# A one-core hybrid decoder layer: its order of issue made with the scheduler's detailed machine model

## The chip, the cores and the metric

The kernel runs on one core of one Trainium2 chip. The metric is the device time of one execution in microseconds (us), lower is better. Five engines work beside each other, each through a queue of its own: TensorE (PE) multiplies, VectorE (DVE) and ScalarE (ACT) do elementwise work, GpSimd (POOL) does almost nothing here, and SyncE (SP) issues DMA transfers; ACT issues some too. Each queue is a fixed list, made when the kernel is built, and an instruction that waits for another engine holds up what stands behind it in its list.

## What is computed

A decoder layer over 2048 rows of 1024 numbers. Two mixing groups read one normalised projection, their outputs go through one output projection, and a gated FFN follows. All is float32. Cut to what matters:

```
h = rms_norm(x, pre_mix_norm)
proj = h @ w_in                       # lru_x, lru_gate, ssd_z, ssd_x, B, C, dt
lx = conv4(lru_x)
lh = rg_lru(lx, ...)                  # gates, then a scan over time
y_lru = rms_norm(lh * gelu(lru_gate))
xbc = silu(conv4(ssd_x, B, C))
dt = softplus(ssd_dt + bias)
y = ssd_chunked(x * dt, dt * A, B, C) # chunks of 128 rows, decays by running sums of dt * A
y_ssd = rms_norm((y + d * x) * silu(ssd_z))
x = x + rms_norm(concat(y_lru, y_ssd) @ w_out)
h = rms_norm(x, pre_ffn_norm)
x = x + rms_norm((silu(h @ w_gate) * (h @ w_up)) @ w_down)
```

## The kernel before

Each float32 operand of a product is split in two: `s_hi`, a cast to the matmul's type on ACT (L132), and `s_lo`, what that cast left out, on DVE (L133). A product is then three matmuls per tile, hi by hi (L137), hi by lo (L138) and lo by hi (L139), on tiles of 128 x 512. The FFN takes seven products where a plain block scheme takes eight, so it works on sums of weight halves (`S`) and on operands built by casts `hx` and `hy` (L717, L718).

The mixing half works on two time blocks of 1024 rows. A block runs its SSD units, eight of them in two groups of four, then its eight LRU units. A unit begins with projections of 48 matmuls each into a PSUM tile `pp` (pool of two); PE does the mixing itself into tiles `pq` (another pool of two). The stretches, as the trace shows them: start 0 to 50 us, SSD of block 0 to 340, LRU of block 0 to 550, the same for block 1 to 830 and 1020, output projection to 1362, FFN gate and up products to 2205, FFN down products to 2634.

The code is written unit by unit, and the Tile framework's scheduler turns it into the five queues: it keeps each dependence and decides, with a model of what instructions cost, which of the ready ones is put next on each engine. The kernel's author steers it in places by a higher priority (`HQ`) and by places (`site`) at which a mixing stage is written between two halves of a projection; no order is written out by hand.

Names that matter below, in the order of the program. At the start three projections (dt, B and C of block 0) run on raw x, since the row norm isn't known yet; L620 squares x on ACT and L167 makes the operands `hx`. L158 spreads the row norms over the partitions on PE and ACT copies them to `rsb`, which every later projection of block 0 is multiplied by on DVE (L295, writing `xr`, from which the convolution reads: L299 on ACT, then taps L302 on DVE). Right behind that copy the code loads eight tiles of x rows for block 1's norm (L632, on SP) and squares them on ACT (L633):

```
rms_of(acc, rtok[:, 0])
a.copy(out=rsb, in_=spread(rtok[:, 0], 0, NC, t4()))                      # L627, L158 within
...
        sy.dma_start(out=xr, in_=x[r0:r0 + P, :])                         # L632
        a.activation(out=xr, in_=xr, func=AF.Square, accum_out=ss[...])   # L633
```

L422 transposes the dt rows into a `pq` tile. The decay chain follows: L443, L447 (running sums on PE), L449 (copy to `Bt` on DVE), a write to DRAM `cs_dr`, loads L511 that spread a row of it over all partitions (`L`), and then per unit: L514 transposes x on PE, L516 and L518 make `t4` from it on DVE, L524 and L525 turn `L` into exponents on DVE, L530 (PE) multiplies `t4`, and L535, L542, L546, L551 carry the chunk states. L118 sums squares over partitions on PE at a block's end. L243, L244 and L172 make operands of later projections.

At 1362 to 1400 the output projection's last rows and the FFN's first products overlap: L717 and L718 build operands, L132, L735 split weights and sums of weights, L917 copies a product out, L920 and L921 (silu) work on it.

## Time and profile before

| what | value |
|---|---|
| time, median of 3 runs | 2635.73 us (2632.55 to 2636.6) |
| the profiled execution's own time | 2635.64 us |
| its span | 2633.8 us |
| PE busy | 2613.7 us, 99% |
| DVE busy | 1852.7 us, 70% |
| ACT busy | 1123.6 us, 43% |
| mean granted TensorE clock | 0.999 of full speed |

The span goes from the first to the last instruction. The profile of this kernel is read on two scales: over the whole, where PE is always busy, and at single places, where the row of time of one engine shows how long it stood still before an instruction and what released it.

### The profile page before, as it was taken

The page shows a single profiled execution, that of the slowest core. Times are in us where ns is not written, and L with a number is a line of the kernel's source. Part 1 is how long each engine was busy: PE and PEld are TensorE (multiplying, and loading weights), DVE is VectorE, ACT ScalarE, POOL GpSimd, SP SyncE. Part 2 cuts the span into 40 slices and gives each one's busy share as a digit, 9 for nine tenths or more (in the row PEclk, how much of TensorE's full clock was granted, in tenths as well). Part 3 has the DMA queues.
Part 4 walks back from the last instruction along what each step waited for, and adds up shares of the span by engine and source line. Part 5 has one row for each costly group of instructions (what it writes and reads, how often), then busy time and mean ns, then how long its engine had stood idle before and what let it go on. Part 6 is the DMA issues. An engine that isn't in the chain of part 4 may idle for free.

```text
span 2633.8 us, 31866 instructions
## 1 busy us (share of the span) xinstructions
PE 2613.7 (99%) x12360; PEld 2170.4 (82%) x12360; DVE 1852.7 (70%) x2716; ACT 1123.6 (43%) x1340; POOL 1.1 (0%) x8
## 2 busy tenths in 40 slices
PE   9999999999999999999999999999999999999998
PEld 7888888888888887888877888888888888888887
DVE  7997878888777767544478777678767675334676
ACT  6544456754535777332253222234222222322443
POOL 0000000000000000000000000000000000000000
PEclk9999999999999999999999999999999999999999
DMA  5342461223334635543454333235333325444664
GB/s 211 111 131 73 128 201 65 82 88 113 95 96 150 210 96 205 154 136 123 143 196 150 134 104 116 81 121 195 104 100 110 106 92 173 151 139 153 212 245 140
DMA packets 189975, 357.79 MB, mean 136 GB/s; under 512 B 18528, under 2 KB 91616, under 8 KB 189824
## 3 DMA queue, kind: packets, MB, share of 16 engines
q1 hardware_dynamic: 88912, 256.56, 30.3%
q10 hardware_dynamic: 100912, 99.20, 10.8%
q8 instruction: 97, 1.59, 0.2%
q14 instruction: 54, 0.44, 0.1%
HBM read 253.86 MB, written 101.84 MB: 135 GB/s over the span
## 4 chain that ended last, share of the span: by engine, by line
PE 93%; DVE 3%; ACT 2%; DMA 1%; issue 1%; DVEq 0%; ACTq 0%; SPq 0%
PE pf L139 16%; PE pf L138 16%; PE pf L137 16%; PE pp L137 11%; PE pp L139 10%; PE pp L138 10%; PE pq L137 3%; PE pq L138 3%; PE pq L139 3%; PE pq L530 1%; PE pq L542 1%; PE pq L551 1%; DMA t_dr<-L 1%; PE pq L514 1%; DVE t L399 0%
## 5 line engine op out<-in xcount | busy, mean ns | idle before, releaser
L137 PE MATMUL pp<-hx,s_hi 128*128 128x512 f32 x1392 | 548.2, 394 | 1.2 <-ACT hx L243 0.7
L139 PE MATMUL pp<-hx,s_lo 128*128 128x512 f32 x1392 | 545.4, 392 | 0.5 <-DVE s_lo L133 0.5
L138 PE MATMUL pp<-hx,s_hi 128*128 128x512 f32 x1392 | 543.6, 391 | 0.6 <-DVE hx L244 0.6
L132 ACT CAST s_hi<-raw 128x1024 fp32r<-128x1024 f32 (+1 forms) x167 | 170.3, 1022 | 380.2 <-PE pp L138 123.0
L139 PEld LDWEIGHTS pp<-hx,s_lo 128*128 128x128 f32 x1392 | 261.7, 188 | 56.5 <-issue 0.9
L137 PEld LDWEIGHTS pp<-hx,s_hi 128*128 128x128 f32 x1392 | 261.8, 188 | 56.2 <-issue 1.6
L138 PEld LDWEIGHTS pp<-hx,s_hi 128*128 128x128 f32 x1392 | 261.9, 188 | 54.2 <-DVE hx L244 1.0
L139 PE MATMUL pf<-hx,s_lo 128*128 128x512 f32 x704 | 273.9, 389 | 0.7 <-DVE s_lo L133 0.7
L137 PE MATMUL pf<-hx,s_hi 128*128 128x512 f32 x704 | 274.2, 389 | 0.4 <-ACT s_hi L132 0.4
L138 PE MATMUL pf<-hx,s_hi 128*128 128x512 f32 x704 | 273.9, 389 | 0.0
L133 DVE TENSOR_TENSOR s_lo<-raw,s_hi 128x1024 fp32r<-128x1024 f32 (+1 forms) x167 | 198.0, 1187 | 64.1 <-ACT s_hi L132 55.7
L978 DVE TENSOR_TENSOR d_lo<-draw,d_hi 128x1024 fp32r<-128x1024 f32 (+1 forms) x110 | 121.5, 1129 | 171.4 <-ACT d_hi L977 170.1
L132 ACT CAST s_hi<-S 128x1024 fp32r<-128x1024 f32 x86 | 90.3, 1050 | 268.6 <-PE pf L138 247.3
L138 PE MATMUL pf<-d_lo,d_hi 128*128 128x512 f32 x504 | 196.1, 389 | 0.0
L977 ACT CAST d_hi<-draw 128x1024 fp32r<-128x1024 f32 (+1 forms) x110 | 104.9, 980 | 213.5 <-PE pf L138 181.6
L139 PE MATMUL pf<-d_hi,d_lo 128*128 128x512 f32 x504 | 195.9, 389 | 0.0
L137 PE MATMUL pf<-d_hi 128*128 128x512 f32 x504 | 194.6, 389 | 0.0
L139 PEld LDWEIGHTS pf<-hx,s_lo 128*128 128x128 f32 x704 | 132.1, 188 | 28.9 <-DVE s_lo L133 1.6
L137 PEld LDWEIGHTS pf<-hx,s_hi 128*128 128x128 f32 x704 | 132.1, 188 | 28.2 <-ACT s_hi L132 0.9
L138 PEld LDWEIGHTS pf<-hx,s_hi 128*128 128x128 f32 x704 | 132.1, 188 | 27.4
L302 DVE SCALAR_TENSOR_TENSOR lx<-xr,pk,lx 128x1024 f32<-128x1024 f32 x108 | 138.2, 1279 | 10.4 <-ACT lx L299 9.3
L138 PE MATMUL pf<-hy,s_hi 128*128 128x512 f32 x356 | 138.8, 390 | 1.5 <-DVE hy L718 1.4
(339 smaller groups left out, 4518.2 us busy)
## 6 DMA issues: line engine op xcount, KB each, us to landing
raw<-w_gu_dram SPq DMA_DIRECT2D x86, 512.0 KB, 4.2
f_dr<-fo ACTq DMA_DIRECT2D x154, 256.0 KB, 4.5
raw<-w_in_dram SPq DMA_DIRECT2D x72, 512.0 KB, 3.4
draw<-f_dr SPq DMA_DIRECT2D x57, 512.0 KB, 4.3
L<-cs_dr SPq DMA_DIRECT2D x32, 512.0 KB, 5.3
g_dr<-t ACTq DMA_DIRECT2D x32, 512.0 KB, 3.4
raw<-g_dr SPq DMA_DIRECT2D x32, 512.0 KB, 5.0
raw<-h_dr SPq DMA_DIRECT2D x26, 512.0 KB, 4.4
```

What stands on the lines that cost most here:

```text
L132: a.copy(out=hi, in_=raw)
L133: v.tensor_sub(out=lo, in0=raw, in1=hi.bitcast(F32))
L137: te.matmul(o, lhsT=wh, rhs=hi, start=start, stop=False)
L138: te.matmul(o, lhsT=wh, rhs=lo, start=False, stop=False)
L139: te.matmul(o, lhsT=wl, rhs=hi, start=False, stop=stop)
L302: v.scalar_tensor_tensor(out=y, in0=xr[:, k:k + TB], scalar=cw(k), in1=y, op0=ALU.mult, op1=ALU.add)
L514: te.transpose(pt[:, c].rearrange("p j d -> p (j d)"), xc[:, c * P:(c + 1) * P], ident)
L530: te.matmul(pst[:, c, :], lhsT=Bt[:, c, :], rhs=xe[:, c].rearrange("p j d -> p (j d)"), start=True, stop=True)
L542: te.matmul(po[:, c, :], lhsT=(sc[:, xi, :] if c == 0 else U[:, c - 1, :]), rhs=C[:, c * P:(c + 1) * P], start=True, stop=True)
L551: te.matmul(py[64 * j:64 * j + 64, c, :], lhsT=xd[:, c, j, :], rhs=L[:, j, c, :], start=True, stop=True)
L977: a.copy(out=hi, in_=r)
L978: v.tensor_sub(out=lo, in0=r, in1=hi.bitcast(F32))
```

## The change

One argument of the framework's context changes. It lets the scheduler weigh its choices on a simulated timeline of the machine in place of a coarser count:

```
-    with tile.TileContext(nc) as tc:
+    with tile.TileContext(nc, schedule_with_timeline_sim=True) as tc:
```

Both kernels have the same 16,501 instructions on the same tiles; loads of ACT's function tables go from 105 to 100, and waits are placed anew. On PE the order differs strongly up to 400 us (mixing matmuls, `pq`, stand further behind the projections, `pp`; 45 matmuls of projections go ahead of L158), a little up to 850, at 980 to 1110, at 1362 to 1400 and at 2200 to 2530, and not at all over 1400 to 2200. SP puts an eighth weight load ahead of the x rows (L632) where it put seven. Three places follow.

ACT's queue at 42 to 56 us, as the difference of the two orders (`t_465` to `t_477` are tiles of x rows, `Cc` and `lx` convolutions):

```order
-L132 CAST s_hi<-raw 128x1024
-L627 COPY rsb<-pq 128x1024
 L633 ACTIVATE t_465,h_ss<-t_465 128x1024
-L299 ACTIVATE lx<-xr,pk 128x1024
 L633 ACTIVATE t_466,h_ss<-t_466 128x1024
 L633 ACTIVATE t_467,h_ss<-t_467 128x1024
-L299 ACTIVATE Cc<-xr,pk 128x1024
+L627 COPY rsb<-pq 128x1024
+L132 CAST s_hi<-raw 128x1024
 L633 ACTIVATE t_468,h_ss<-t_468 128x1024
 L633 ACTIVATE t_477,h_ss<-t_477 128x1024
+L299 ACTIVATE lx<-xr,pk 128x1024
```

The copy to `rsb` has gone behind three squares of x rows, and the first convolutions behind two more.

DVE's queue around the first unit's decays, at 82 to 96 us, before (numbers tell tiles apart):

```order
L449 COPY Bt_580<-pq_571 16x1024
L490 TENSOR_TENSOR SM_611<-pq_602,tri_138 128x1024
L302 SCALAR_TENSOR_TENSOR lx_855<-xr_853,pk_109,lx_855 128x1024 x2
L516 TENSOR_TENSOR t4_760<-pq_751,dt_525 128x1024
L302 SCALAR_TENSOR_TENSOR lx_855<-xr_853,pk_109,lx_855 128x1024
L518 TENSOR_TENSOR t4_762<-t4_760,ed_585 128x1024
L524 TENSOR_TENSOR L_748<-L_748,cs_583 128x2048
L535 SCALAR_TENSOR_TENSOR t4_835<-sc_149,aet_588,pq_826 128x64
L525 TENSOR_SCALAR L_748<-L_748 128x2048
```

and now:

```order
L449 COPY Bt_580<-pq_571 16x1024
L133 TENSOR_TENSOR s_lo_1073<-raw_1070,s_hi_1072 128x1024
L490 TENSOR_TENSOR SM_611<-pq_602,tri_138 128x1024
L524 TENSOR_TENSOR L_748<-L_748,cs_583 128x2048
L302 SCALAR_TENSOR_TENSOR lx_855<-xr_853,pk_109,lx_855 128x1024
L516 TENSOR_TENSOR t4_760<-pq_751,dt_525 128x1024
L524 TENSOR_TENSOR L_954<-L_954,cs_583 128x2048
L525 TENSOR_SCALAR L_748<-L_748 128x2048
L302 SCALAR_TENSOR_TENSOR lx_855<-xr_853,pk_109,lx_855 128x1024
L518 TENSOR_TENSOR t4_762<-t4_760,ed_585 128x1024
L525 TENSOR_SCALAR L_954<-L_954 128x2048
```

The first L524 stands ahead of L516 and L518 of its unit where it stood behind them, and a second L524, that of the next unit, is there too.

PE's queue where the mixing of block 0's seventh unit begins, at 266 to 270 us, before:

```order
L542 MATMUL pq_2104<-Cc_1574,sc_149 128x128
L542 MATMUL pq_2104<-Cc_1574,t4_2021 128x128 x7
L551 MATMUL pq_2116<-L_1934,t4_1946 64x128 x16
L514 MATMUL pq_2144<-ident_113,lx_2041 128x128 x8
L137 MATMUL pp_2164<-hx_214,s_hi_1960 128x512
```

and now, from the row behind L551 on:

```order
L139 MATMUL pp_2256<-hx_341,s_lo_2053 128x512
L137 MATMUL pp_2256<-hx_345,s_hi_2052 128x512
L138 MATMUL pp_2256<-hx_346,s_hi_2052 128x512
L139 MATMUL pp_2256<-hx_345,s_lo_2053 128x512
L137 MATMUL pp_2256<-hx_349,s_hi_2052 128x512
L138 MATMUL pp_2256<-hx_350,s_hi_2052 128x512
L139 MATMUL pp_2256<-hx_349,s_lo_2053 128x512
L137 MATMUL pp_2256<-hx_353,s_hi_2052 128x512
L138 MATMUL pp_2256<-hx_354,s_hi_2052 128x512
L139 MATMUL pp_2256<-hx_353,s_lo_2053 128x512
L137 MATMUL pp_2405<-hx_214,s_hi_2167 128x512
L514 MATMUL pq_2144<-ident_113,lx_2041 128x128 x8
```

The transposes L514 into `pq_2144` stood right behind L551; now eleven matmuls of projections stand between.

## Rows read from the trace of the kernel before

**Rows 1.** The page: busy us (share), instructions; the chain's shares; one matmul group.

```profile
PE 2613.7 (99%) x12360; PEld 2170.4 (82%) x12360; DVE 1852.7 (70%) x2716; ACT 1123.6 (43%) x1340; POOL 1.1 (0%) x8
...
PE 93%; DVE 3%; ACT 2%; DMA 1%; issue 1%; DVEq 0%; ACTq 0%; SPq 0%
...
L138 PE MATMUL pp<-hx,s_hi 128*128 128x512 f32 x1392 | 543.6, 391 | 0.6 <-DVE hx L244 0.6
```

**Rows 2.** FFN stretch: its length, each engine's busy us (instructions), clock, DMA.

```profile
1500.00:1600.00 100.00, 100.00 (x443) 82.81 (x442) 71.49 (x102) 28.92 (x38) 0.00 (x0) 1.00 0.28 95
```

**Rows 3.** PE's timeline: start, us, instruction, [idle before, releaser].

```profile
269.25 1.06 PE L514 MATMUL pq<-ident,lx 128*128 128x128 f32 x8 [1.75 <-DVE t L546]
...
389.06 0.50 PE L138 MATMUL pq<-t,bd 128*128 128x512 f32 x1 [0.78 <-DVE t L378]
...
547.51 1.95 PE L118 MATMUL pq<-ones,acc 128*128 128x1 f32 x16 [0.97 <-DVE acc L322]
...
1002.11 0.50 PE L138 MATMUL pp<-hx,s_hi 128*128 128x512 f32 x1 [0.56 <-DVE hx L244]
...
1011.10 0.50 PE L137 MATMUL pp<-hx,s_hi 128*128 128x512 f32 x1 [0.67 <-ACT hx L243]
```

**Rows 4.** Stretches behind two of these stalls; the clock stands third from the end.

```profile
551.00:555.00 4.00, 4.00 (x12) 3.09 (x12) 3.76 (x21) 3.11 (x5) 0.00 (x0) 0.60 0.36 131
...
268.00:274.00 6.00, 4.75 (x25) 4.13 (x26) 5.96 (x6) 0.24 (x1) 0.00 (x0) 1.00 0.82 240
```

**Rows 5.** ACT's timeline around rsb.

```profile
48.11 1.02 ACT L627 COPY rsb<-pq 128x1024 f32<-128x1024 f32 x1 [4.77 <-PE pq L158]
50.69 1.06 ACT L633 ACTIVATE t<-t 128x1024 f32<-128x1024 f32 x1 [1.56 <-DMA t<-x_dram]
```

**Rows 6.** The chain at 44 us; transfer rate over 0 to 75 us.

```profile
44.07 6.59 DMA t<-x_dram
...
GB/s 5 221 337 397 388 405 398 404 400 420 409 256 11 0 4 48 232 0 0 0 0 0 4 249 205 323 393 417 411 417 422 223 24 0 0 0 0 0 9 0
```

**Rows 7.** PE's timeline, start and decay chain.

```profile
49.27 1.07 PE L422 MATMUL pq<-ident,Bt 128*128 128x128 f32 x8
...
79.61 0.46 PE L443 MATMUL pq<-dtx,tri 128*128 128x128 f32 x2 [1.14 <-DVE halo L300]
```

**Rows 8.** DVE's timeline behind the decay chain; SP's loads; the page on them.

```profile
82.18 1.21 DVE L449 COPY Bt<-pq 16x1024 f32<-16x1024 f32 x1 [1.26 <-PE pq L447]
...
90.98 1.27 DVE L302 SCALAR_TENSOR_TENSOR lx<-xr,pk,lx 128x1024 f32<-128x1024 f32 x1
92.17 1.22 DVE L518 TENSOR_TENSOR t<-t,ed 128x1024 f32<-128x1024 f32 x1
93.31 2.28 DVE L524 TENSOR_TENSOR L<-L,cs 128x2048 f32<-128x2048 f32 x1
...
95.80 1.22 DVE L525 TENSOR_SCALAR L<-L 128x2048 f32<-128x2048 f32 x1
...
85.33 1.76 SPq L511 DMA_DIRECT2D L<-cs_dr  x4
...
L<-cs_dr SPq DMA_DIRECT2D x32, 512.0 KB, 5.3
```

**Rows 9.** Stretches of block 0; DVE's busy time is the third.

```profile
100.00:120.00 20.00, 20.00 (x127) 16.91 (x125) 18.80 (x28) 11.88 (x11) 0.00 (x0) 1.00 0.34 106
...
220.00:240.00 20.00, 20.00 (x129) 17.14 (x128) 13.78 (x27) 9.18 (x9) 0.00 (x0) 1.00 0.12 37
```

**Rows 10.** The chain: one product in two units of block 0.

```profile
127.39 1.90 PE pq L551 x32
...
155.80 1.90 PE pq L551 x32
```

**Rows 11.** PE's timeline where the FFN begins.

```profile
1380.61 0.50 PE L138 MATMUL pf<-hy,s_hi 128*128 128x512 f32 x1 [1.16 <-DVE hy L718]
...
1390.74 0.50 PE L137 MATMUL pf<-hx,s_hi 128*128 128x512 f32 x1 [0.44 <-ACT s_hi L132]
```

## The prediction

> **What bounds the kernel now.** I read the page's busy shares first, then its chain of work, then TensorE's own row of time, since a new order can only win where an engine that sets the end stands still. PE is busy 2613.7 us of a span of 2633.8, and the chain that ended last is 93% PE [rows 1]. The reader is to see two things there. First, all idle time of PE together is 2633.8 − 2613.7 = 20.1 us, 0.76% of the span: no order of the same instructions can win more than that, apart from what the clock gives. Second, VectorE is at 70% over the whole, so wherever it is much fuller than that it can become what PE waits for.
>
> Next I read the stretches. In the FFN (1362 to 2634 us) PE is busy 100.00 us of 100 and issues 443 matmuls in them [rows 2], one every 0.226 us; DVE stands at 71.49 there. No order can help in it. The Trainium skill, "Perfetto Trace Analysis", section "Identifying the Most-Contended Engine", says that matmul busy time is a poor measure of how near TensorE is to its limit and takes weight-load busy time in its place; that is 82.81 of 100 in the same row, which by the Trainium skill would leave 17% of room. The row decides for me: PE waits nowhere in that stretch, so the room, if there is any, is not one that an order opens.
>
> What is left are PE's stalls, and these are few [rows 3]. The idle time before a matmul, which the timeline puts in brackets, is 1.75 us at 269.25 (eight transposes of the mixing stage wait for VectorE's L546), 0.78 at 389.06 (and as much again at 510.95 us), 0.97 at 547.51, 0.56 at 1002.11 and 0.67 at 1011.1 us. Behind the one at 547.51 the granted clock is 0.60 over 551 to 555 us, while behind the longer one at 269 it stays at 1.00 [rows 4]. The start of the kernel is the other place where PE waits for something other than PE.
>
> **The change part by part.** Instructions, tiles and pools stay; only the place of each instruction in its engine's queue changes. An engine takes its queue in turn, so what matters is who now stands behind whom. The profiled execution took 2635.64 us, of which 2633.8 are span and 1.8 lie outside it; the median of the three runs is 2635.73, so sums made on the trace carry over as they stand.
>
> *Gains.* In the new order the projection's matmuls (pp) stand ahead of the mixing stage's (pq) that wait for VectorE: at 269 us, 11 matmuls of 0.226 us now stand between L551 and the transposes, and the L542 whose result L546 reads are begun earlier too, and counted in PE work the wait's end is far behind. I walked each of the six stalls against the new queues, and all six have their releaser done before PE arrives. Idle time 1.75 + 0.78 + 0.78 + 0.97 + 0.56 + 0.67 = 5.5 us [rows 3]; the first matmul after a stall also takes 0.50 us [rows 3] where such matmuls take 0.391 on average [rows 1], which makes 0.1 each and 6.2 in all. If the clock's fall at 551 goes with the stall before it, 4 us × (1 − 0.60) = 1.6 us more [rows 4].
>
> *Start.* On ACT, L627 (the copy that makes rsb, the row norms spread over all partitions) ran at 48.11 us, and the first square of an x row (L633) at 50.69, having waited 1.56 us for its DMA [rows 5]. Now three squares stand ahead of L627. The first row lands at 44.07 + 6.59 = 50.7 us [rows 6]; rows of 512 KB at some 410 GB/s [rows 6] follow 1.28 us apart, so the third lands at 53.2. The square takes 1.06 us and L627 1.02 [rows 5], so rsb is ready at about 55.4 rather than 49.1. SyncE's queue also has one more weight load ahead of these rows, which puts up to 1.28 us on it: 55.4 to 56.7, and I take 56.1, 7 us later.
>
> What covers that? PE moves 45 projection matmuls (10.2 us) ahead of L158, whose result rsb copies, so PE is at its transposes L422 at about 53.1 and not at 49.27 [rows 7], with that much more of its later work done. They need rsb (it frees their PSUM buffer): a stall of 56.1 − 53.1 = 3.0 us, 2.3 to 3.6 by the bounds above. Everything on VectorE that multiplies by rsb (L295) moves late by about 7 us too.
>
> *The decay chain.* By the walk PE's L447 of the first block ends at 93.0, and L449 takes 1.21 us [rows 8]. From L449's end at 83.39 it was 1.94 us to SyncE's loads L511 (issued 85.33), which take 5.3 to land [rows 8]: L is there at 94.2 + 1.9 + 5.3 = 101.4 us. Before, VectorE did L516 and L518, of which the next PE product L530 is made, and then L524, the first to need L. Now L524 stands ahead of L516, so L518 waits for the load, and two L524 (2.28 each), one L525 (1.22), two L302 (1.27), L516 and L518 (1.22, both of one shape) [rows 8] are 10.8 us and make it end at about 112.2; PE arrives at 108.1 by the walk: a stall of 4.1 us, or 4.7 if its load waits for a weight load's tail. The wait of 1.14 us at 79.61 [rows 7] goes, with its slow first matmul 1.3. To these comes 0.2 us at the very start, where a square (L620) steps ahead of the first L167. Start and decay chain: 0.2 + 3.0 + 4.4 − 1.3 = +6.3 us.
>
> *What follows.* VectorE cannot win this back soon: it is busy 18.80 of 20 us at 100 us, about the same in each 20 us up to 200, and 13.78 at 220 [rows 9]. One unit of the SSD loop took 155.80 − 127.39 = 28.4 us [rows 10]. By the new queues the loop from one L295 to the next is a projection of 48 matmuls (10.9 us) and some 1.8 us of mixing on PE, then about 16.8 us on VectorE, an estimate from the durations above: 29.3 us. That puts 0.9 us on each of the first two units, before VectorE has room: +1.8. So the first block loses 8 us; I hold 5 to 11 for it, from 2.3 of stall and no growth to a growth over five units.
>
> *Output projection to FFN, 1378 to 1396.* The casts of hy go ahead on both engines, so the gap of 1.16 us at 1380.61 [rows 11] and three smaller ones in the 5 us behind it go, 2.4 us in all by my count of that stretch. But the cast L132 of the FFN's first weight sums, which ended a wait of 0.44 us at 1390.74 on PE [rows 11], now stands behind the silu L921 of a later product. PE is there at 1387.2 by the walk and is served at about 1390.7: 3.5 us, with 0.6 for the second half 4.1, of which 1.3 (this wait, the like one at 1392 and their slow first matmuls) were there before. Net 4.1 − 1.3 − 2.4 = +0.4, bounds −1.3 and +2.
>
> *Rest.* New small waits in the LRU stage and the second block, where the walk leaves under 1.5 us of slack: +1, bounds 0 and +2.5.
>
> *The clock.* The new stalls are of 3, 4 and 3.5 us. Behind the stall of 0.97 us at 547.51 the clock fell for 1.6 us' worth; behind 1.75 us at 269 it did not [rows 3, 4]. The Trainium skill, "TensorE: Matmul & The Clock Gate", section "HAM oscillation — how this bites in real kernels", has idle gaps on PE bring the clock back down, which speaks against this change: it trades several short gaps for few long ones. By the rule all three would pay 1.6 us; the trace agrees at 547 and not at 269. By the rows, then, each pays 0 or 1.6, and I take one of three in full.
>
> **The sum.** −6.2 − 1.6 + 8 + 0.4 + 1 + 1.6 = +3.2 us, by the bounds −3 to +13. On 2635.7 that is 2639.
>
> **The rivals.** *It is slower beyond what can be measured.* One mechanism: rsb late, VectorE behind it and full until 200 us. If the loop's 29.3 us hold through five units and not two, the loss of the first block is 11 us, and if the clock falls behind all three stalls another 3.2: +3.2 + 3 + 3.2 = +9.4, 2645; with both PE stalls at their far ends 2648. For it speaks that VectorE has 1.2 us to spare in 20; against it that some VectorE work (L133 for weights far ahead) has room to slip. It decides from where PE at 230 us is more than 10 us behind the old order.
>
> *It is faster.* If PE has enough finished projections to run over the late rsb (its two pp buffers and the 45 matmuls speak for it, the two buffers' release by L295 against it), the start costs 2 us and not 8: −3, about 2633, not yet measurable; with VectorE's order closer than I walked and no clock fall −6 or more, 2627 to 2630. A third would be that PE's matmuls themselves run closer together, by more than the 20.1 us of idle: under 2614. That is what the Trainium skill's measure of headroom would allow; nothing in the rows supports it, and I give it 1 in 100.
>
> *It does nothing.* The queues in the FFN and the tail keep their order on PE, half the kernel, and PE always has the same 2613.7 us of work. Then gains and losses cancel to within 2 us: 2634 to 2638. The forecast differs from it only by size.
>
> **How the numbers follow.** About 0.2% (5.3 us) is what a measurement of this kernel can tell from no change: 2630.5 to 2641. My forecast, a small loss inside that band, together with the case of nothing, holds 0.49; the slower rival 0.40; faster beyond the band 0.11. The likeliest time is 2639. The range runs from 2629 (half of the faster case) to 2650 (the far end of the slower one); the likeliest case alone would be 2633 to 2643.
>
> **What would show it.** In the trace after: rsb (L627) ends at 55 to 57 us and not at 49.1; PE has a stall of about 3 us before L422 and one of about 4 before the first L530; a stall of about 3.5 us near 1390; none at the six places above; VectorE over 95% busy to about 240 us; the lag of PE against the old order some 8 us at 230, some 3 at 1400 and unchanged to the end. I am wrong if rsb comes before 52 us, if VectorE keeps pace so that the lag at 230 is under 4 us, or if the FFN stretch, with PE's order the same, takes another time than 443 matmuls in 100 us.

## The result, and the profile after

The new order takes 2662.1 us (median of 4 runs, 2661.2 to 2663.4) against 2635.8: a ratio of 1.0103, interval 1.0085 to 1.012. It is 26.4 us slower. The sign was the forecast's, a loss; the size was not, and the time lies outside the range.

The page of the new order, with the lines that answer to [rows 1]: busy us (share) and instructions by engine, then the chain by engine.

```profile
span 2659.4 us, 31893 instructions
...
PE 2622.9 (99%) x12360; PEld 2179.0 (82%) x12360; DVE 1849.9 (70%) x2716; ACT 1124.9 (42%) x1335; POOL 1.1 (0%) x8
...
PE 91%; DVE 4%; ACT 2%; DMA 2%; issue 1%; ACTq 0%; SPq 0%; DVEq 0%
```

The shares hardly changed, and PE still reads 99%. Two differences make up the whole result. PE stands still for 2659.4 − 2622.9 = 36.5 us where it was 20.1, +16.4. And the same matmuls keep it busy for 2622.9 us where it was 2613.7, +9.2, since some run at the lower clock. Together 25.6 us, the difference of the spans.

PE's timeline of the new order, all idle times over 1.5 us after the first 55 (start, us, instruction, [idle before, releaser]); it answers to [rows 3, 7 and 11]:

```profile
55.25 1.06 PE L422 MATMUL pq<-ident,Bt 128*128 128x128 f32 x8 [1.52 <-ACT rsb L627]
...
110.05 3.42 PE L530 MATMUL pq<-t,Bt 128*128 128x128 f32 x16 [3.63 <-DVE t L518]
...
145.35 0.50 PE L137 MATMUL pp<-hx,s_hi 128*128 128x512 f32 x1 [2.32 <-DVE xr L295]
...
345.67 0.79 PE L137 MATMUL pp<-hx,s_hi 128*128 128x512 f32 x1 [4.10 <-DVE xr L295]
...
405.68 0.73 PE L137 MATMUL pq<-t,bd 128*128 128x512 f32 x2 [2.96 <-ACT t L377]
...
407.92 0.79 PE L137 MATMUL pp<-hx,s_hi 128*128 128x512 f32 x1 [1.51 <-DVE t L308]
...
1056.86 0.73 PE L137 MATMUL pq<-wob,s_hi 128*128 128x512 f32 x2 [2.93 <-ACT wob L243]
...
1414.19 0.80 PE L137 MATMUL pf<-hx,s_hi 128*128 128x512 f32 x1 [4.88 <-ACT s_hi L132]
```

These eight are 23.9 us of idle time. The old order had none over 1.75 in these stretches.

Stretches of the new order (length, busy us of PE, PEld, DVE, ACT, POOL with their instructions, clock, DMA share, GB/s); they answer to [rows 2, 4 and 9]:

```profile
100.00:120.00 20.00, 16.37 (x80) 13.99 (x79) 20.00 (x17) 8.16 (x6) 0.00 (x0) 0.91 0.33 108
120.00:140.00 20.00, 20.00 (x123) 16.67 (x121) 13.35 (x24) 5.71 (x6) 0.00 (x0) 1.00 0.51 132
...
220.00:240.00 20.00, 20.00 (x98) 16.81 (x97) 19.25 (x18) 13.06 (x11) 0.00 (x0) 1.00 0.28 93
...
110.00:114.00 4.00, 3.95 (x21) 3.90 (x22) 4.00 (x4) 3.04 (x3) 0.00 (x0) 0.63 0.00 0
...
146.00:150.00 4.00, 4.00 (x19) 3.30 (x18) 4.00 (x7) 2.04 (x3) 0.00 (x0) 1.00 0.39 131
346.00:350.00 4.00, 4.00 (x13) 3.15 (x13) 4.00 (x6) 2.07 (x3) 0.00 (x0) 0.69 0.25 81
...
406.00:410.00 4.00, 2.49 (x7) 1.69 (x6) 4.00 (x6) 3.35 (x4) 0.00 (x0) 0.56 0.48 135
410.00:414.00 4.00, 4.00 (x12) 3.09 (x12) 4.00 (x6) 3.25 (x4) 0.00 (x0) 0.58 0.95 331
1057.00:1061.00 4.00, 3.43 (x9) 2.43 (x10) 2.65 (x5) 3.65 (x5) 0.00 (x0) 0.68 0.96 325
...
1415.00:1419.00 4.00, 4.00 (x10) 3.09 (x10) 4.00 (x6) 1.03 (x2) 0.00 (x0) 0.50 0.33 123
...
1600.00:1700.00 100.00, 100.00 (x443) 82.81 (x442) 71.34 (x102) 29.40 (x37) 0.00 (x0) 1.00 0.27 93
```

The last row is that of [rows 2] again: 443 matmuls in 100 us, the FFN is untouched. Behind the stalls of 2.9 us and more the clock is low; behind 2.32 at 145 it is not in this trace (the last section has others). The loss (1 − clock) × 4 us is 1.5 at 110, 1.2 at 346, 3.4 at 406 to 414, 1.3 at 1057 and 2.0 at 1415, with the two stretches behind the last two (0.89 and 0.84) another 1.1: 10.5 us. The 1.6 at 551 in the old order is gone, which leaves 8.9, about the 9.2; part of the slow clock lies in idle time, where it costs nothing.

To see where the time was lost I compared, matmul by matmul, when the two traces had issued the same amount of PE work. The difference is PE's *lateness*; it changes only where one of the kernels stalls or runs slow. "Lateness" below is always this number, worked out from one trace of each kernel. Matmuls of unlike size have to be weighed for it, so it is good to some 0.3 us, and two executions of one order can differ by more, as the last section shows.

| stretch, us | lateness at its end | change | predicted |
|---|---|---|---|
| 0 to 225 | 9.6 | +9.6 | +8 (start) |
| 225 to 325 (stall at 269 gone) | 7.7 | −1.9 | a gain |
| 325 to 375 | 13.9 | +6.2 | in "Rest" |
| 375 to 400 | 14.4 | +0.5 | in "Rest" |
| 400 to 425 (here the product that waited at 389) | 21.0 | +6.6 | in "Rest", and a gain |
| 425 to 550 | 19.7 | −1.3 | a gain |
| 550 to 600 (clock at 551) | 16.8 | −2.9 | a gain |
| 600 to 1000 | 17.7 | +0.9 | in "Rest" |
| 1000 to 1050 | 16.4 | −1.3 | a gain |
| 1050 to 1100 | 21.8 | +5.4 | in "Rest" |
| 1100 to 1400 | 21.7 | −0.1 | 0 |
| 1400 to 1450, then flat to the end | 25.3 | +3.6 | +0.4 |

The gains came: 1.9 + 1.3 + 2.9 + 1.3 = 7.4 us where the sum had 6.2 + 1.6 = 7.8, of which 0.9 was for the wait at 389. That product comes at 419 in the new order and doesn't wait, but its gain cannot be seen apart beside the loss at 405. The start came in size. What the sum had put at +1, the "Rest", is +6.2 + 0.5 + 6.6 + 0.9 + 5.4 = 19.6 us: three places of which the prediction knew nothing, at 345, 405 and 1057 us.

**345 us.** DVE's and ACT's timelines of the new order, where PE waits for L295:

```profile
340.92 1.23 DVE L370 TENSOR_TENSOR SM<-L,bd 128x1024 fp32r<-128x1024 f32 x1 [5.62 <-ACT bd L365]
342.06 1.22 DVE L322 TENSOR_TENSOR acc<-acc,t 128x1024 f32<-128x1024 f32 x1
343.20 1.28 DVE L302 SCALAR_TENSOR_TENSOR lx<-xr,pk,lx 128x1024 f32<-128x1024 f32 x1
344.39 1.22 DVE L295 TENSOR_TENSOR xr<-pp,rsb 128x1024 f32<-128x1024 f32 x1
```

```profile
329.72 1.40 ACTq L362 DMA_DIRECT2D L<-wa_dram  x2
...
338.99 1.90 ACT L365 CAST bd<-L 128x2048 fp32r<-128x2048 f32 x1 [10.33 <-DMA L<-wx_dram]
```

The gate weights of the LRU stage are loaded into `L`, a tile that the SSD stage's decays use too. The loads are issued 29 us later than in the old order, where the cast L365 ran at 312.0:

```profile
300.49 1.40 ACTq L362 DMA_DIRECT2D L<-wa_dram  x2
```

The new order kept the cast and its user at the head of their queues all the same: ACT stands 10.33 us, DVE 5.62, and L295, which is ready and which PE needs, stands three places behind.

**1057 us.** ACT's timeline shows the same with another load:

```profile
1053.00 1.05 ACT L132 CAST s_hi<-raw 128x1024 fp32r<-128x1024 f32 x1 [5.14 <-DMA raw<-g_dr]
...
1055.14 1.04 ACT L132 CAST s_hi<-raw 128x1024 fp32r<-128x1024 f32 x1 [1.09 <-DMA raw<-g_dr]
1056.09 0.72 ACT L243 ACTIVATE wob<-raw,pk 128x512 fp32r<-128x512 f32 x1
```

### The profile page after: what moved, and what is told of

Read it like the earlier page. It is cut to its first block, busy times and chain, and to the rows that moved or that the text cites. A ratio compares the mean times of both kernels' runs of the same rounds, so it can differ in the third digit from the quotient of the medians.

```text
span 2659.4 us, 31893 instructions
## 1 busy us (share of the span) xinstructions
PE 2622.9 (99%) x12360; PEld 2179.0 (82%) x12360; DVE 1849.9 (70%) x2716; ACT 1124.9 (42%) x1335; POOL 1.1 (0%) x8
## 4 chain that ended last, share of the span: by engine, by line
PE 91%; DVE 4%; ACT 2%; DMA 2%; issue 1%; ACTq 0%; SPq 0%; DVEq 0%
PE pf L137 16%; PE pf L138 15%; PE pf L139 15%; PE pp L137 11%; PE pp L138 11%; PE pp L139 11%; PE pq L138 2%; PE pq L139 2%; PE pq L137 2%; PE pq L551 1%; PE pq L542 1%; PE pq L530 1%; DMA L<-cs_dr 1%; PE pq L761 0%; DVE lx L302 0%
## 5 line engine op out<-in xcount | busy, mean ns | idle before, releaser
L132 ACT CAST s_hi<-raw 128x1024 fp32r<-128x1024 f32 (+1 forms) x167 | 170.4, 1023 | 346.4 <-PE pf L138 124.9
L132 ACT CAST s_hi<-S 128x1024 fp32r<-128x1024 f32 x86 | 90.6, 1054 | 341.2 <-PE pf L138 316.6
L302 DVE SCALAR_TENSOR_TENSOR lx<-xr,pk,lx 128x1024 f32<-128x1024 f32 x108 | 138.1, 1279 | 5.3 <-ACT lx L299 4.7
```

The costliest lines, as they stand in the source:

```text
L132: a.copy(out=hi, in_=raw)
L302: v.scalar_tensor_tensor(out=y, in0=xr[:, k:k + TB], scalar=cw(k), in1=y, op0=ALU.mult, op1=ALU.add)
```

## The experiments

Each kernel below has all instructions and tiles of both kernels and an order of issue written out in full; only the places named differ. Where two orders are joined at a time t, the first part is what started before t in that order's own trace, and the rest follows in the other order.

**Which half loses? The new order to 250 us, then the old one:**

```
-0 to end: new order
+0 to 250 us: new order; the rest: old order
```

> The order of the changed kernel up to 250 us of its trace (start and six SSD units of block 0), the order of the kernel before for all the rest, written out instruction by instruction. Theory P (each place pays for its own order): TensorE is 9.6 us late at 230 us, as in the changed kernel, and loses nothing behind that, since the order there is the old one: no stall of 3 us or more at 345, 405, 1057 or 1414 us; the old stalls near 511, 547, 1002 and 1380 us are back. Time 2645 us (2642 to 2648). Theory Q (the late start leaves a backlog in VectorE and the mixing stages, which bursts when the LRU units begin): the stalls at 345 and 405 us come all the same, 12.6 us with their clock: 2658 us.

It took 2652.7 us (1.007, 1.0055 to 1.0085). Lateness is 11.5 at 225 us, 17.7 at 350 and 18.9 at the end, with no stall at 345, 405, 1057 or 1414. So those four places belong to the later part of the order, as theory P had it, and the start alone loses some 11 us here. The time is above theory P's 2642 to 2648 all the same, for 6 us are the join's: PE stands still before the transposes that the new order had put off, with the clock at 0.79 over 284 to 292 us.

```profile
285.57 1.79 PE L514 MATMUL pq<-ident,lx 128*128 128x128 f32 x8 [4.44 <-DVE t L546]
```

**The other way round, the old order to 240 us, then the new one:**

```
-0 to end: new order
+0 to 240 us: old order; the rest: new order
```

> The other half: the order of the kernel before up to 240 us of its trace, the order of the changed kernel for all the rest. Theory P: no loss at 230 us, but the stalls where the LRU units of block 0 begin (4.3 and 4.8 us with the clock's share 12.6), before the output projection (5.6) and before the FFN (3.6) stand, and the gains near 269, 547 and 1002 us too: 26.4 less 9.6, 2652 us (2649 to 2656). Theory Q: without the late start the stalls at 345 and 405 us are gone or under 1 us each: 2640 us (2637 to 2643).

2652.6 us (1.0067, 1.0052 to 1.0082). PE is not late at 230 (−0.7) and still stands in all the later places:

```profile
334.03 0.80 PE L137 MATMUL pp<-hx,s_hi 128*128 128x512 f32 x1 [2.89 <-DVE xr L295]
...
394.16 0.73 PE L137 MATMUL pq<-t,bd 128*128 128x512 f32 x2 [3.00 <-ACT t L377]
...
1047.90 1.22 PE L137 MATMUL pq<-wob,s_hi 128*128 128x512 f32 x2 [3.27 <-ACT wob L243]
...
1405.84 0.80 PE L137 MATMUL pf<-hx,s_hi 128*128 128x512 f32 x1 [4.88 <-ACT s_hi L132]
```

Lateness at the end is 15.8, and the time is in theory P's range. The later stalls are no echo of the late start, as theory Q had it: they come with the order behind 240 us alone.

**The start: is it the late rsb?** The new order with L627 ahead of the three squares and L158 ahead of the 22 projection matmuls that the new order has before it:

```
 L91 ACTIVATE rs_s<-rs_v 128x8
+L627 COPY rsb<-pq 128x1024
 L633 ACTIVATE t_465,h_ss<-t_465 128x1024
 L633 ACTIVATE t_466,h_ss<-t_466 128x1024
 L633 ACTIVATE t_467,h_ss<-t_467 128x1024
-L627 COPY rsb<-pq 128x1024
```

> The changed kernel's order with the start undone in two rows: on ACT the copy to rsb (L627) goes back ahead of the three squares of x rows (L633), and on PE the two matmuls of the spread (L158) go back ahead of the 22 projection matmuls that the change put there. Theory of the prediction (late rsb starts the loss): rsb ends near 50 us and not at 55.1, the stall of 1.7 us before L422 goes, VectorE is 5 us earlier, the stall of 3.8 us at 110 us shrinks to under 1, and TensorE is 3 to 4 us late at 230 us where it was 9.6: 2655 to 2656 us. Rival (the loss sits in VectorE's own order, L524 ahead of L516 and L518, which waits for the decays): only the first stall goes, 1.7 us: 2660 us.

2663.5 us (1.0114, 1.0098 to 1.0129), no gain. The stall at 55 is gone, but PE stands 1.67 us at 67.5 for L295, and the one at 110 is still 3.5. Lateness at 230 is 7.95 instead of 9.6. Executions of one order differ by as much (last section), so no gain is shown for the late rsb, which the prediction put first and priced at 3 us. The new order's own trace agrees: its lateness is 1.8 us at 70, behind this stall, and 0.1 at 100, before the stall at 110.

**The start: is it the decay tiles?** L516 and L518 ahead of the first L524, as in the old order:

```
+L516 TENSOR_TENSOR t_760<-pq,dt 128x1024
+L518 TENSOR_TENSOR t_762<-t_760,ed 128x1024
 L524 TENSOR_TENSOR L<-L,cs 128x2048
 L302 SCALAR_TENSOR_TENSOR lx<-xr,pk,lx 128x1024
-L516 TENSOR_TENSOR t_760<-pq,dt 128x1024
```

> The changed kernel's order with one row of VectorE undone: L516 and L518 of the first SSD unit, which make what the PE product L530 reads, go back ahead of the two L524, which wait for the load of the decays. Theory V (the start's loss is a VectorE queue whose head waits for a load): L518 ends at about 100 us and not at 109.9, the stall of 3.8 us before L530 at 110 us goes, and TensorE is 4 to 5 us less late at 230 us, where it was 9.6: 2656 to 2658 us. Rival (the decay chain itself is late, since PE's sums L443 and L447 stand behind projections: L447 came at 90 us and not at 80): the stall moves on to the next product that needs the decays, L551 or the next unit's L530, and the lag at 230 us stays over 8 us: 2661 to 2662 us.

The time did not fall, 2667.7 us (1.0124, 1.0109 to 1.014), above both theories. The stall at 110 is gone, and L295, now behind those two, makes a longer one:

```profile
113.58 0.80 PE L137 MATMUL pp<-hx,s_hi 128*128 128x512 f32 x1 [5.30 <-DVE xr L295]
```

Lateness at 230 is 10.4. DVE has no room at that place (20.00 of 20 us at 100 to 120, above): to put one thing first only changed what PE waits for.

**The gate weights at 345 us**, behind what is ready, on DVE and likewise L365 on ACT (behind L321 and L299):

```
+L322 TENSOR_TENSOR acc<-acc,t_2155 128x1024
+L302 SCALAR_TENSOR_TENSOR lx<-xr,pk,lx 128x1024
+L295 TENSOR_TENSOR xr<-pp,rsb 128x1024
+L302 SCALAR_TENSOR_TENSOR lx<-xr,pk,lx 128x1024
+L133 TENSOR_TENSOR s_lo<-raw,s_hi 128x1024
 L370 TENSOR_TENSOR SM<-L,bd 128x1024
```

> The changed kernel's order with the wait at 345 us undone: VectorE's first L370, which waits for ACT's cast of the gate weights (L365), goes behind the L295 that frees a projection's PSUM tile, and on ACT that cast, which waits 10.3 us for the load of the gate weights, goes behind L321 and L299. The weights themselves come no earlier. Theory H (a ready L295 stands behind L370): the 4.3 us stall at 345 us and the slow clock behind it go, 5.9 us: the lag at 370 us is 8 and not 13.6, 2656 us. Rival (the whole LRU stage is late because its weights are): the stall at 345 us goes but those at 405 and 408 us grow by as much: 2660 to 2662 us.

The stall is gone. The stretch of 340 to 360 us, first of the new order and then of this kernel:

```profile
340.00:360.00 20.00, 15.90 (x76) 13.24 (x75) 15.50 (x29) 11.01 (x11) 0.00 (x0) 0.91 0.33 106
```

```profile
340.00:360.00 20.00, 20.00 (x123) 16.95 (x123) 16.05 (x31) 8.45 (x9) 0.00 (x0) 1.00 0.37 119
```

Lateness at 375 is 7.75 instead of 13.9, and 14.5 instead of 21.0 at 425. That is the whole +6.2. The stalls at 405 and 408 came as long as before (3.01 and 1.51 us), so the rival's mechanism is out. Yet the time, 2660.7 us (1.0102, 1.0088 to 1.0116), can't be told from the new order's 1.0103: by 1075 us the lateness is 22.3, for PE now also stands near 898 us, and the step at 1057 is 6.5.

**The place at 405 us.** On DVE L302 ahead of the scan L399 and L308 ahead of L397; on ACT one L310 and two L571 behind L377:

```
+L302 SCALAR_TENSOR_TENSOR lx<-xr,pk,lx 128x1024
 L399 SCALAR_TENSOR_TENSOR t_2697<-t_2699,hc,t_2697 128x1024
-L302 SCALAR_TENSOR_TENSOR lx<-xr,pk,lx 128x1024
 L567 TENSOR_TENSOR L<-L 128x512
+L308 TENSOR_TENSOR t_2966<-pp,rsb 128x1024
 L397 SCALAR_TENSOR_TENSOR t_2884<-t_2884,lx 128x1024
```

> The new order with one place changed, at 390 to 410 us. On DVE the convolution L302 goes ahead of the scan L399 and L308 ahead of L397; on ACT one L310 with its table load and two L571 go behind the cast L377 that PE waits for. In the new order PE waits there 2.96 us for L377 and 1.51 us for L308, and its lateness against the old order grows by 6.7 us. Theory Q, places in the queues: L377 starts at about 403.9 instead of 404.6 and L308 ends at 405.5 instead of 407.9; the stalls are 2.2 and 0, the step about +4, the time some 2.5 us below the new order's. Theory D, debt: PE computed the gates of the LRU stage's first units late (374 us where the old order had them at 339), so that two units' chains of gate product, L386, L390, L391, L393 follow each other within 20 us, and the last of them holds L377 up by its buffer; what was put behind it is then late in its turn: the step stays at +6 or more, the time within 1.5 us of 2661.

One stall of the two is left, of the length that places in the queues gave:

```profile
406.80 0.74 PE L137 MATMUL pq<-t,bd 128*128 128x512 f32 x2 [2.11 <-ACT t L377]
```

The stretch of 400 to 425 us in this kernel:

```profile
400.00:425.00 25.00, 22.89 (x101) 18.49 (x100) 25.00 (x28) 22.98 (x22) 0.00 (x0) 1.00 0.59 196
```

The new order has the clock at 0.86 over the same 25 us and PE busy for 20.52; here it is 1.00 and 22.89. Lateness grows by about 1 us and not 6.6: 2.4 us of idle time and 25 × 0.14 = 3.5 of clock are saved. So by the trace it was places in the queues (theory Q), and the debt theory falls for all but the stall that is left. The time stayed at 2661.5 us (1.0105, 1.0087 to 1.0122), where theory D had it, but its four runs lie between 2656.3 and 2667.3 and can't tell 2.5 us. The traced execution is already 14.2 us late at 225, with the order up to there unchanged, and the steps at 899, 1057 and 1414 remain.

**The places at 1057 and 1414 us**, both in one kernel. On ACT two `wob` copies, and a copy of a product (L806) between them, go ahead of the casts that wait for a load, and at 1414 the cast of the weight sums ahead of the silu (with the sums themselves ahead of L935 on DVE):

```
+L243 ACTIVATE wob<-raw,pk 128x512
+L806 ACTIVATE mx<-pp,r 128x1024
+L243 ACTIVATE wob<-raw,pk 128x512
 L132 CAST s_hi<-raw 128x1024 x2
-L243 ACTIVATE wob<-raw,pk 128x512
-L806 ACTIVATE mx<-pp,r 128x1024
 L806 ACTIVATE mx<-pp,r 128x1024
-L243 ACTIVATE wob<-raw,pk 128x512
...
+L132 CAST s_hi<-S 128x1024 x2
 L944 DMA f_dr_0_91<-fo 128x512
 L921 ACTIVATE fu<-fu 128x512
-L132 CAST s_hi<-S 128x1024 x2
```

> The changed kernel's order with two places undone. At 1057 us the ACT cast of an output weight (L243, wob_7678, and the one behind it) goes ahead of the two casts (L132) that wait for a load from DRAM, with its VectorE partner (L244). At 1414 us the four VectorE sums of FFN weights (L728 to L732) go ahead of the work queued there, and the two ACT casts of them (L132) ahead of the silu L921. Theory H (an engine's queue: a ready cast stands behind one that waits): the 3.1 us stall at 1057 and the 4.8 us stall at 1414 fall under 0.5 and 1.5 us, and the clock does not drop behind them: 5 and 3 to 3.6 us less than the changed kernel, 2653 to 2654 us. Theory L (the load itself, and the DVE's amount of work, are late): PE stops one or two matmuls later for the same time: 2660 to 2662 us.

2660.3 us (1.0093, 1.0076 to 1.011). The two places answer differently:

```profile
901.54 0.50 PE L137 MATMUL pq<-t,bd 128*128 128x512 f32 x1 [1.67 <-ACT t L377]
903.70 0.50 PE L138 MATMUL pq<-t,bd 128*128 128x512 f32 x1 [1.66 <-DVE t L378]
...
1063.00 0.50 PE L137 MATMUL pp<-hx,s_hi 128*128 128x512 f32 x1 [2.94 <-ACT s_hi L132]
...
1416.05 0.50 PE L137 MATMUL pf<-hx,s_hi 128*128 128x512 f32 x1 [1.94 <-ACT s_hi L132]
```

At 1057 the stall moved on by 6 us, to the product of the casts that wait for the load. ACT's timeline of this kernel shows what held them up:

```profile
1061.29 0.72 ACT L243 ACTIVATE wob<-raw,pk 128x512 fp32r<-128x512 f32 x1 [4.86 <-DMA acc_dr<-acc]
1061.92 1.98 ACT L132 CAST s_hi<-raw 128x1024 fp32r<-128x1024 f32 x2
```

The two loads landed 6.0 and 7.0 us after their issues at 1051.85 and 1053.18, so at 1057.9 and 1060.2, and the casts ran only at 1061.92 and 1062.9, behind the second `wob` copy, which waited 4.86 us for a store. The edit put one wait at the head of ACT's queue in place of another. So this run doesn't decide between the theories at 1057: it doesn't show that the load itself is too late for PE, and no run had the first copy alone moved. At 1414 the stall fell from 4.88 to 1.94 and the step from +3.6 to −0.3, so there it was the place. What was gained was lost near 902 (+5.4).

**Several places at once.** First the decay products (L443 to the first L514) 21 matmuls earlier on PE, with the places at 345 and 1414:

```
+L443 MATMUL pq<-dtx,tri 128x128
+L444 MATMUL pq<-dtx,ones 128x128
 (21 matmuls pp, L137 to L139)
-L443 MATMUL pq<-dtx,tri 128x128
-L444 MATMUL pq<-dtx,ones 128x128
```

> The changed kernel's order with three places undone at once, each to be read at its own time in the trace. (1) On PE the first unit's decay sums and transposes (L443, L444, L447, L482, L488, L514) go 21 projection matmuls, 4.8 us, further ahead, to where VectorE has L436 ready for them (83.7 us). (2) The gate weights' cast and difference (L365, L370) behind L299 and L295, as in fix_gate. (3) The sums of FFN weights and their casts ahead of the queued work, as in fix_act. Theory M (the change puts mixing matmuls off on PE; VectorE and ScalarE stand idle for it and are too full afterwards to make it up): VectorE's idle 5.75 us before L454 at 89 us goes, the stall of 3.8 us at 110 us falls under 1, TensorE is 4 to 6 us late at 230 us and not 9.6; with 5.9 for (2) and 4 for (3): 2662.1 less 14, 2648 us (2646 to 2652). Rival (the first block is bound by VectorE's amount of work): the stall moves on to the next unit, the lag at 230 stays over 8, and the sum is 2652 to 2654 us.

2651.2 us (1.0066, 1.0052 to 1.0079). The three gave 1.2 us of lateness at 225 (8.4 for 9.6), 5.8 at 345 (+0.4 for +6.2) and 5.2 at 1414 (−1.6 for +3.6). The time is theory M's, but not its account of the start, which had lateness at 4 to 6 us by 230 (the rival: over 8): 1.2 us is less than executions of one order differ by. At the start PE then waits 0.44 us before L530 at 108.6, but 1.12 at 96.8 for L484 on ACT, and still 2.32 at 142.5, for L295. Then all four, with the place at 405:

```
 (the edits of the last kernel)
+(the edits at 405 us)
```

> The new order with all four of its places changed at once: the decay products 21 matmuls earlier on PE, the gate weights' casts behind what was ready (345 us), the place at 405 us, and the sums of the FFN's weights ahead (1414 us). The first, second and fourth together gave 2651.2 us. Theory Q (places in the queues): 2.5 less, 2648.7. Theory D (debt): the same as without the third, 2650 to 2652.5. Either way the start's loss of some 8 us by 230 us stays, so that it is not below 2643.

2649.7 us (1.0057, 1.004 to 1.0074), between the two theories, and the interval overlaps that of the last kernel. In the trace lateness grows by 3.5 us over 375 to 425 where the last kernel had 6.8 (both places are earlier there by up to 6 us, so the stretch is wider), but near 900 PE now loses 4.0 instead of 2.2, and the start 10.4 instead of 8.4. With all four places mended the new order is still 15 us behind the old.

**Which stretch of the new order is worth having?** The old order with the new one's 399 to 580 us, where its stalls at 511 and 547 were:

```
-0 to end: old order
+0 to 399 us: old; 399 to 580: new; the rest: old
```

> The order of the kernel before up to 399 us of its trace, of the changed kernel up to 580 us of its trace, and of the kernel before for the rest: it takes from the change only the stretch in which TensorE caught up 4.6 us (20.2 us late at 500 us, 16.6 at 580), with the waits of 0.78 us at 511 and 0.97 at 547 and the slow clock behind it gone. If gains and losses are each their place's own (theory P): 2635.5 less 4 to 4.6, 2631 us. If the gains there are only lateness caught up by mixing work that the change had put off (theory Q): 2635 to 2636 us, no difference.

2632.1 us against 2633.3 in the same comparison (0.9996, 0.9987 to 1.0005): no difference that can be told. PE is 6.0 us ahead of the old order at 550, 4.2 at 600, 3.7 at 1000 and 2.1 from 1050 to the end. The stall at 405 is not in this stretch: the product that waits there stands at 387.9 in the old order's trace, before the join. The same with the new order's 240 to 295 us, where the stall at 269 was:

```
+0 to 240 us: old; 240 to 295: new; to 399: old; 399 to 580: new; the rest: old
```

> As best1, and from 240 us of the trace of before to 295 us of that of after also the changed order, where TensorE caught up 1.9 us. Theory P: 2629 us. Theory Q: what the stretch puts off has to be done right behind it, in the old order, and PE waits there for VectorE as it did at 285 us in the kernel that went back at 250: 2 to 4 us are lost again, 2631 to 2635 us.

2647.8 us (1.0055, 1.0042 to 1.0067):

```profile
291.44 3.75 PE L530 MATMUL pq<-t,Bt 128*128 128x128 f32 x16 [3.67 <-DVE t L518]
...
301.57 3.10 PE L542 MATMUL pq<-Cc,t 128*128 128x128 f32 x14 [3.04 <-DVE t L535]
...
310.64 1.94 PE L514 MATMUL pq<-ident,lx 128*128 128x128 f32 x8 [2.90 <-DVE t L546]
```

The lateness goes from −2.3 at 275 to +14.4 at 325. In those 55 us the new order runs projections early and puts mixing steps off; when the old order takes over, the mixing chain is short of its lead, and PE waits for DVE at three links of it. Last, the first of these two, with L514 of two units only 8 and 4 matmuls later, and the new order at 1362 to 1430 us with the FFN's sums ahead:

```
+L137 MATMUL pp_2164<-hx_214,s_hi_1960 128x512
+ (7 more matmuls pp)
 L514 MATMUL pq_2144<-ident_113,lx_2041 128x128 x8
- (the same 8 matmuls)
```

> As best1 (old order; changed order from 399 us of before to 580 us of after), with three more edits: the transposes L514 of the seventh unit of block 0 stand 8 projection matmuls later and those of one unit of block 1 4 later, where VectorE is not done with what frees their buffer; and from 1362 to 1430 us the changed order, with the sums of FFN weights and their casts ahead. If each place's stall is its own and a delay of 1 to 2 us of mixing work costs nothing behind it: 2632 less 0.5 to 1.7 at 268 us and 1 to 2.5 at 1380 to 1396, 2629 us (2627 to 2631). If small delays of mixing work are paid back behind, as large ones are: 2631 to 2633 us, no difference from best1.

2629.1 us against 2633.7 (0.9986, 0.9977 to 0.9995): faster than the old order by 0.14%, as the first theory had it. Its lateness is −6.5 from 1400 us to the end, and its span 2627.3 us.

## Why the prediction was wrong

**Right.** The gains (7.4 of 7.8 us), stall by stall but for the one at 389. The FFN: 443 matmuls in 100 us, lateness flat from 1450 to the end. The start in size (+9.6 for +8, within 5 to 11; some 1.5 of it is slow clock, which the sum counts apart), and in one of its two waits: L530 waits 3.63 us for L518, where the sum had 4.1 to 4.7; L518 ended at 109.9, not 112.2, and PE was there at 106.4, not 108.1.

**The start in its parts.** rsb ended at 55.1 against 56.1, as ACT's timeline shows beside [rows 5], and PE stood for 1.52 us and not 3.0, which was made up by 100 us; neither the run with rsb nor that with the decay tiles put back was faster. So the start's size came in part by luck: +1.9 up to there (0.2 + 3.0 − 1.3) came to 0.1, and 9.5 us were lost behind. PE in the new order begins its decay products late although their operand is there. ACT's, PE's and DVE's timelines of the new order, at rsb and at the decay products:

```profile
54.12 0.99 ACT L627 COPY rsb<-pq 128x1024 f32<-128x1024 f32 x1
```

```profile
88.54 0.38 PE L443 MATMUL pq<-dtx,tri 128*128 128x128 f32 x2
```

```profile
83.44 0.29 DVE L436 TENSOR_TENSOR dtx<-dt,amat 128x128 f32<-128x128 f32 x1
...
89.48 0.29 DVE L454 TENSOR_TENSOR ed<-pq,cs 128x128 f32<-128x128 f32 x1 [5.75 <-ACT cs L452]
...
108.69 1.22 DVE L518 TENSOR_TENSOR t<-t,ed 128x1024 f32<-128x1024 f32 x1
```

L443 starts 4.8 us after its operand is ready; in the old order L443 began 0.1 us after L436 ended [rows 7]:

```profile
79.19 0.28 DVE L436 TENSOR_TENSOR dtx<-dt,amat 128x128 f32<-128x128 f32 x1
```

In the new order DVE meanwhile stands idle for 5.75 us, and is full 10 us later. Those products 21 matmuls earlier, with two other edits, left lateness at 8.4, so this isn't shown to be the cause either. The growth of the loop by 0.9 us per unit, held through two units or, in the slower rival, five, isn't there: the lateness is flat from 175 us (9.2) to 275 (9.4). (Its terms add up to 29.5 us and not 29.3, and the sum's low bound to −4.1 and not −3; nothing hangs on either.) What the sum put under growth was mostly one stall, 2.32 us at 145. And "VectorE over 95% busy to about 240 us" did not come: it was busy 20.00 of 20 us at 100 but 13.35 at 120. No single edit took the start's loss away, so its one cause, if there is one, stays open.

**The step that failed: "Rest", "where the walk leaves under 1.5 us of slack: +1, bounds 0 and +2.5".** It was +19.6. My walk through the queues carried durations and matmuls but took each load to be there when its user came up. At 345 and 1057 ACT waits for a load (10.33 and 5.14 us at the head of its queue), and what PE needs stands behind. At 405 DVE works from 397 to 414 us without a gap, so whatever was put ahead of L302 and L308 there is paid for in full. The kernels with one place mended show 345 and 405 to be places in queues. At 1057 the wait at the head of ACT's queue is seen, but whether the place or the load itself costs the 5.4 us stays open.

**Output projection to FFN.** The wait was seen (the cast L132 behind the silu L921) and its price was 4.1; it is 4.88 us, at 1414 in the new order's time. The gain of 2.4 from the gaps that go did not show apart, the clock fell behind the stall (0.50, then 0.84), and +0.4 became +3.6.

**The clock.** I counted three stalls and took one at 1.6. It is five places and 10.5 us; as −1.6 for 551 came true, the net is +8.9 where the sum had 0. The Trainium skill ("TensorE: Matmul & The Clock Gate", section "HAM oscillation — how this bites in real kernels") has long idle gaps on PE bring the clock back down; the trace agrees for each of these five, of 2.9 us or more. The fall on which the prediction's price rests came behind a short gap, 0.97 us at 547, and that is not what the section tells of.

**The rival that was right in sign** (slower) named the wrong mechanism: VectorE was not full to 200 us (13.35 of 20 at 120), and the loop did not grow. Its deciding point, a lateness above 10 us at 230, doesn't decide: it was 9.6 here, but 11.5 and 14.2 at 225 in two other kernels with the same order up to there. More than half of the net loss came later, from places no rival named. "It does nothing" fails with them.

## What to carry to other kernels

When only the order changes, look on each engine for the instructions whose operand comes by DMA or by a buffer that others free late, and ask what stands behind them; a term called "the rest" is worth a walk of its own before it gets a price. An order that begins matmul work early has taken the place of something that it puts off, and the bill comes where that is needed, as the 55 us from 240 to 295 show, which cost 17. Price a stall with what the clock does behind it: in the new order's trace the stalls of 2.9 us and more cost about half as much again.

## What the runs showed that I had not expected

- The clock behind a stall does not go by the length of the stall alone, nor by the order. In the new order it is 0.50 to 0.69 of full speed over the next 4 us behind stalls of 2.9 us and more (the lower level of 1.2 GHz for most of it) and 1.00 behind 1.52 and 2.32. It is 1.00 behind 1.75 us in the old order, but 0.60 behind the 0.97 us at 547 [rows 4]. And the same wait of 2.32 us for L295 that left it at 1.00 at 145 came at 148.32 in the kernel with the place at 405 changed, and was followed by:

```profile
148.00:152.00 4.00, 3.68 (x10) 2.96 (x11) 4.00 (x6) 2.24 (x2) 0.00 (x0) 0.64 0.38 122
```

- Two stalls close together are dear: 2.96 and 1.51 us around 406 cost 4.5 of idle time and 3.4 of clock, and in all seven kernels that kept this place the clock is 0.57 to 0.60 over the 8 us from the first. With the second stall mended, 2.11 us left the clock at 1.00 in one kernel (at 406.8) and at 0.57 over 402 to 406 us in another (at 400.8, all four places mended).
- The same order of the first 225 us gave a lateness there of 8.8, 9.2, 9.6, 11.5 and 14.2 us in five kernels. Most of this spread is the granted clock: its mean over 50 to 225 us is 0.99, 0.98, 0.99, 0.97 and 0.96, a loss of about 1.7, 3.4, 1.7, 5.1 and 6.8 us, and without it 7.1, 5.8, 7.9, 6.4 and 7.4 are left. A difference of 1 or 2 us at the start, between single traces, shows nothing.
- A stall near 900 us, of 1.1 to 3.3 us of idle time, came in all eight kernels with a place mended or a first part exchanged that kept the new order there, though not in the new order's own profile. In each of the eight, 8 to 10 us before it, DVE waits 0.9 to 2.3 us for a store to land, and ACT, whose next work waits for that DVE row, stands still for 3.3 to 4.7 us; in the new order's own profile DVE has no such wait there and ACT stands for 2.5. In the kernel with the gate weights moved:

```profile
888.39 0.69 DVE L566 TENSOR_TENSOR L<-L 128x512 f32<-128x512 f32 x1 [1.57 <-DMA t_dr<-L]
```

  The store lands 4.8 to 6.2 us after its issue in the eight, and 4.3 in the new order's own profile. Why is not known. All eight have their order written out, and no run has the new order written out unchanged, so whether the writing out plays a part is not tested.
